# Four raw units leave the down projection for the gate and up units, and a raw unit's two dot products are parted

## The chip, the core and the metric

The kernel runs on one core of a Trainium2 chip. A core has TensorE (PE, matmul), VectorE (DVE), ScalarE (ACT), GpSimd (POOL) and SyncE (SP, which issues most DMAs here), each with its own queue of instructions, and 16 DMA engines that they share. The metric is the device time of one execution in microseconds, lower is better; the number given is the median of three runs.

## The reference

A decoder trunk of two layers on 256 tokens of width 1024, in float32. Each layer has a token mixer (convolution and retention) and a channel part: a dense SwiGLU of width 2816 in layer 0, experts in layer 1. Shift, scale and gate vectors come from a conditioning vector c. Cut to what matters here:

```python
c_act = silu(c)
for l in range(2):
    ada = c_act @ w_ada[l] + b_ada[l]          # (1024,) @ (1024, 6144)
    shift1, scale1, gate1, shift2, scale2, gate2 = split(ada, 6)
    h = x * (1 + scale1) + shift1
    x = layer_norm(alpha * x + gate1 * token_mixer(h, ...))
    h = x * (1 + scale2) + shift2
    ff = (silu(h @ w_gate) * (h @ w_up)) @ w_down      # layer 0; layer 1: experts
    x = layer_norm(alpha * x + gate2 * ff)
```

## The kernel before

The kernel streams 490 MB of weights through the core as a sequence of units. A unit is one DMA of up to 128 x 2048 float32 (1 MiB) into one of four buffers, the tile `wf` (NWF = 4), and is worked off in pieces of 128 x 1024. For each piece of a matmul unit ScalarE casts a high part (`wh`, L1696), VectorE subtracts to get the low part (`wl`, L1698), and TensorE multiplies high by high, high by low and low by high. There are six split buffers of each kind (NWS = 6).

A raw unit is not split. Those of `ada_cols` (L258) hold 2 x 1024 columns of `w_ada`, transposed: VectorE multiplies each half by silu(c), kept in `cb` on all partitions, and sums it (L264, with a short read of the accumulator), so that a raw unit is two dot products of 128 x 1024 in a row; the eighth of a group also adds a bias (L273). `ada_pair` makes eight such units for a shift and a scale vector: eight of layer 0 run in the first mixer, and sixteen of layer 1 run in the dense SwiGLU of layer 0. (The first eight of the program, made at L709, are others.)

The order of all work is written out by the program. `prog` is a list of units and code. The loop at its end (L1705) takes one piece after the other: it writes the splitting of pieces up to `look` pieces ahead (`split_to`, L1713; a raw unit counts as one piece), then what was deferred to this piece (`run_deferred`, L1714), then the piece's own work. `look` is 3 for the gate-up units and raws of the dense SwiGLU, 4 for its down units, 2 for the units `RO` of the first mixer. `issue_dma` (L1668) writes the next units' loads on SP's queue, in program order, each as soon as the unit that was issued four before it has been written as consumed: a matmul unit when its last piece is split, a raw unit behind its dot products. Which of the four buffers a load gets, and so what it waits for when it runs, is settled by the framework.

The dense SwiGLU (`ffn`, L993): two units for the first 256 columns, twenty gate-up units `GU_unit(j)`, j = 2 to 21, of two pieces each (called unit j below; 24 matmuls of 256 columns a piece), and twelve down units (22 pieces, 12 matmuls of 512 columns each). A gate-up unit ends with silu (ACT L1046), product (DVE L1047), cast (ACT L1048) and low part of the activation (DVE L1049). The raws are called raw 0 to raw 15. `weave` (L436) puts raws among the gate-up units at an even rate; the last NREST = 4 of the sixteen are kept back (L1064) and put behind the first four down units (L1072):

```python
rest = [r[0] for r in raws[len(raws) - NREST:]]
del raws[len(raws) - NREST:]
weave(units, raws, WFF)
```

In the first mixer the eight raws stand among the last gate units `F` and the units `RO`; the conv norm (`conv_ln`, L776) is deferred to the piece behind the eighth of them.

Of the kernel before, what the change touches and what calls it, by code (L numbers as in the profile page):

```python
# [17 lines left out]
ALU = mybir.AluOpType  # L18
# [4 lines left out]
D = 1024  # L23
# [46 lines left out]
COJ = 0  # L70
MS = (2, 3)
LK = {'A': 5, 'F0': 4, 'F1': 4, 'GUm': 5, 'QK0': 4, 'RO0': 2, 'D': 4}
NREST = 4
SPARE = 6
WFF = 0
START = tuple((w, k) for k in range(8) for w in "as")
# [40 lines left out]
def _emit(tc, ctx, a):  # L117
    nc = tc.nc
    pe, dve, act, pool, sp = nc.tensor, nc.vector, nc.scalar, nc.gpsimd, nc.sync
# [27 lines left out]
    class Unit:  # L147
        kind = None

        def __init__(self, src, n, fn, raw=False, look=LEAD, slot=("stream", "wf", NWF)):  # L150
            self.src, self.n, self.fn, self.raw = src, n, fn, raw
            self.look, self.slot, self.lo = look, slot, {}
            self.issued, self.before = False, None

        def width(self, s):
# [15 lines left out]
    adac = keep.tile([P, L, 48], F32, name="adac")  # L171
# [3 lines left out]
    state = {}  # L175
# [70 lines left out]
    def cook_cb():  # L246
        cb = state.pop("raw_cb", None)
        if cb is not None:
            act.activation(cb, cb, AF.Silu)
# [5 lines left out]
        dve.tensor_scalar(col("taps", 0, L * 8 * CK), col("taps", 0, L * 8 * CK), 0.5, None, op0=ALU.mult)  # L255
        act.activation(ca, col("c", 0, 8), AF.Silu)

    def ada_cols(l, n, k, done=None):  # L258
        def fn(i, w, _):
            cook_cb()  # L260
            for j in range(2):
                wj = w[:, j * D:(j + 1) * D]
                c0 = (n + j) * 8 + k
                dve.scalar_tensor_tensor(wj, wj, 1.0, state["cb"], op0=ALU.mult, op1=ALU.mult,  # L264
                                         accum_out=adac[:, l, c0:c0 + 1])
            if done is not None:
                done()
        return Unit(a["adat"][l, n // 3, k], 2048, fn, raw=True)

    def ada_pair(l, n):  # L270
        def done():
            o = adac[:, l, n * 8:n * 8 + 16]
            dve.tensor_tensor(o, o, adab[:, l, n * 8:n * 8 + 16], op=ALU.add)  # L273
        return [[ada_cols(l, n, k, done if k == 7 else None)] for k in range(8)]

    ada_open = {}

# [37 lines left out]
    def defer(k, fn):  # L315
        deferred.append([k, fn])

    def run_deferred():
        for d in list(deferred):
            d[0] -= 1  # L320
            if d[0] <= 0:
                deferred.remove(d)
                d[1]()
# [112 lines left out]
    def weave(units, raws, after=0, spare=0):  # L436
        n_units = sum(isinstance(u, Unit) and not u.raw for u in units)
        rate = min(1.0, len(raws) / max(1, n_units - after - spare))
        cnt = put = 0
        for u in units:  # L440
            prog.append(u)
            if isinstance(u, Unit) and not u.raw:
                cnt += 1
                while raws and int((cnt - after) * rate + 1e-6) > put:
                    prog.extend(raws.pop(0))
                    put += 1
        for r in raws:
            prog.extend(r)
        raws.clear()

    def mixer(l, raws, bound, fill=(), tail=()):
# [251 lines left out]
        if l == 0:  # L703
            code(open_pool)
            code(lambda: state.update(hp0=R["hp"]))
            code(setup)
            for what, k in START:
                if what == "a":
                    u = ada_cols(0, 0, k, first_h(k))  # L709
                    u.look = 0  # L710
                    if k == ROPE:
                        code(lambda: rope_tables(R["hp"]))
                else:
                    u = S_unit(k)
                prog.append(u)
            code(lambda: R.update(y=keep.tile([P, 8, T], F32, name="ycv", tag="z")))
            code(setup_late)
        else:
            first, t0, second, t1, close = bound
            prog.extend(first)  # L720
            code(t0)
            prog.extend(second)
            code(lambda: state.update(second_tile=t1))
            prog.append(V_unit(0, 0))
            prog[-1].look = 2
            if BEF[1] >= 0:
                prog[-1].before = (first + second)[BEF[1]]
            code(lambda: state.update(turned=lambda: (close(), open_pool())))
            prog.append(V_unit(0, 1))
            units += [A_unit(i) for i in range(6)]  # L730
# [262 lines left out]
    def ffn(raws, bound):  # L993
# [43 lines left out]
        def GU_unit(j):  # L1037
            def fn(s, w, wl):
                if s == 0:
                    R["g"] = mm_bank()  # L1040
                ws_block(R["g"][:, s * T:(s + 1) * T], w, wl, state["hH"], state["hL"], 0, 8, True, True)
                if s == 1:
                    ps = R["g"]
                    sg = R["p"].tile([P, T], F32, name="sg", bufs=2)
                    aa = R["p"].tile([P, T], F32, name="aa", bufs=2)
                    act.activation(sg, ps[:, 0:T], AF.Silu)  # L1046
                    dve.tensor_tensor(aa, sg, ps[:, T:2 * T], op=ALU.mult)  # L1047
                    act.copy(R["aH"][:, j, :], aa)  # L1048
                    dve.tensor_tensor(R["aL"][:, j, :], aa, R["aH"][:, j, :], op=ALU.subtract)  # L1049
            return named('GUf', Unit(a["ffn_gu"][j - 2], 2048, fn))  # L1050
# [12 lines left out]
        units = [GU_unit(j) for j in range(2, KF)]  # L1063
# [3 lines that stand above are left out]
# [564 lines left out]
    late = {}  # L1631
    ada_chunk(0, 2, gate0, lambda: late["p"].tile([P, 512], F32, name="asb", tag="tap", bufs=2))
    mixer(0, ada_pair(0, 3), None, gate0)
    ffn(ada_pair(1, 0) + ada_pair(1, 3), boundary((0, 5), 4))
    opening = []
    mixer(1, [], boundary((1, 2), 1), tail=[lambda: opening[0]()])
# [3 lines left out]
    for u in prog:  # L1640
        if isinstance(u, Unit) and u.look == LEAD and not u.raw:
            u.look = LK.get(u.kind, LEAD)
        if isinstance(u, Unit) and u.kind in LOP:
            n, r, m = LOP[u.kind]
# [13 lines left out]
    consumed = set()  # L1658
# [9 lines left out]
    def issue_dma(upto=None):  # L1668
        while st["dma"] < (len(units) if upto is None else upto):
            u = order[st["dma"]]  # L1670
            where, tag, bufs = u.slot
            p = state.get(where)
            mine = used.setdefault((where, tag, id(p)), [])
            if p is None or not st["go"] or (len(mine) >= bufs and mine[-bufs] not in consumed):
                return
            mine.append(u.idx)
            live.append(p)
            u.wf = p.tile([P, 2048], F32, name="wf", tag=tag, bufs=bufs)
            for o in range(0, u.n, 1024 if u.idx < 2 else u.n):
                o = slice(o, min(u.n, o + 1024) if u.idx < 2 else u.n)  # L1680
                sp.dma_start(u.wf[:, o], u.src[:, o])
            u.w = {}
            u.issued = True
            st["dma"] += 1

    def split_to(i, eng=dve):
        while st["split"] <= min(i, len(subs) - 1):
            u, s = subs[st["split"]]
            if not u.issued:
                return  # L1690
            if not u.raw:
                w = stream.tile([P, 1024], F32R, name="wh", tag="wh", bufs=NWS)
                wl = stream.tile([P, 1024], F32R, name="wl", tag="wl", bufs=NWS)
                m = u.width(s)
                src = u.wf[:, s * 1024:s * 1024 + m]
                act.copy(w[:, 0:m], src)  # L1696
                eng = u.lo.get(s, eng)
                eng.tensor_tensor(wl[:, 0:m], src, w[:, 0:m], op=ALU.subtract)  # L1698
                u.w[s] = (w, wl)
                if s == u.pieces() - 1:  # L1700
                    consumed.add(u.idx)
            st["split"] += 1
            issue_dma()

    for it in prog:  # L1705
        if not isinstance(it, Unit):
            it()
            issue_dma()
            continue
        for s in range(1 if it.raw else it.pieces()):  # L1710
            i = pos_of[it.idx, s]
            st["cur"] = i
            split_to(i + it.look if st["hold"] is None else min(i + it.look, st["hold"] + NWS - 1))  # L1713
            run_deferred()  # L1714
            if it.raw:
                it.fn(0, it.wf, None)
                consumed.add(it.idx)
                issue_dma()
            else:
                it.fn(s, *it.w[s])  # L1720

# [107 lines left out]
```

## Time and profile before

| | |
|---|---|
| median of 3 runs | 1744.8 us (1744.21 to 1747.59) |
| the profiled execution: time | 1747.31 us |
| the profiled execution: span | 1745.4 us |
| TensorE busy | 1693.2 us (97%) |
| VectorE busy | 1548.4 us (89%) |
| ScalarE busy | 1159.6 us (66%) |
| mean granted TensorE clock | 0.991 |
| DMA, mean over the span | 282 GB/s |

The page gives each engine's busy time; a busy TensorE is not TensorE at its peak, since matmuls overlap. Where it matters what holds TensorE up, the views to read are those of one stretch: the windows (busy time of each engine in it), the waits (who waited for whom) and the timeline (each instruction, with the idle time before it and what ended that). In this execution the gate-up units run from about 399 to 514 us, the down units from 514 to 575 us, and the raws of the first mixer from 258 to 313 us.

### The profile page before, as it was taken

Reading aid. Unit: us, or ns where it says so; the run is one execution under the profiler, and the core shown is the slowest. Engines: PE = TensorE matmul, PEld = TensorE weight load, DVE = VectorE, ACT = ScalarE, POOL = GpSimd, SP = SyncE. Lnnn points to the kernel's source line nnn. Section 1 sums busy time; section 2 is a strip of 40 time slices with the busy share of each in tenths; the row PEclk is TensorE's granted clock in tenths of the full one; section 3 lists DMA queues with packets and bytes.
Section 4 is the critical chain, followed back from the end, with each engine's and each line's share of the span. In section 5 each row is a group of like instructions: output and inputs, shape, how many; then the busy total and the mean of one; then the engine's idle time right before and its main releaser. Section 6 shows DMA issues by size and latency. Waiting matters only on the chain. (4 is left out here: it accounts for less than half of the span.)

```text
span 1745.4 us, 23910 instructions
## 1 busy us (share of the span) xinstructions
PE 1693.2 (97%) x8896; PEld 1424.0 (82%) x8896; DVE 1548.4 (89%) x2144; ACT 1159.6 (66%) x1634; POOL 53.3 (3%) x50
## 2 busy tenths in 40 slices
PE   6999999999999999999999999999999999999996
PEld 5988877669997798888887788888888888887885
DVE  7699989877787779999878999899999999898996
ACT  3566787644444565667645878778887878787783
POOL 5300000000000000000000000000000000000001
PEclk8999999999999999999999999999999999999998
DMA  9644458876789544455577799899998999898892
GB/s 358 260 164 161 166 208 295 309 294 230 299 303 353 205 171 161 154 192 174 189 301 290 304 333 389 306 383 361 370 363 329 382 354 383 310 393 308 323 351 86
DMA packets 71389, 491.59 MB, mean 282 GB/s; under 512 B 7985, under 2 KB 8753, under 8 KB 14178
## 3 DMA queue, kind: packets, MB, share of 16 engines
q1 hardware_dynamic: 69410, 484.29, 74.0%
q0 software_dynamic: 1568, 5.45, 0.9%
q8 instruction: 72, 1.18, 0.3%
q14 instruction: 51, 0.42, 0.1%
q10 hardware_dynamic: 288, 0.26, 0.0%
HBM read 488.92 MB, written 1.05 MB: 281 GB/s over the span
## 5 line engine op out<-in xcount | busy, mean ns | idle before, releaser
L1698 DVE TENSOR_TENSOR wl<-wf,wh 128x1024 fp32r<-128x1024 f32 x819 | 977.4, 1220 | 80.1 <-ACT wh L1696 66.0
L1696 ACT CAST wh<-wf 128x1024 fp32r<-128x1024 f32 x819 | 840.9, 1049 | 169.3 <-PE ps_mm L140 102.7
L140 PE MATMUL ps_mm<-wh,hgH 128*128 128x512 f32 x704 | 283.5, 403 | 0.0
L140 PE MATMUL ps_mm<-wh,hgL 128*128 128x512 f32 x704 | 275.8, 392 | 0.0
L140 PE MATMUL ps_mm<-wl,hgH 128*128 128x512 f32 x704 | 275.2, 391 | 0.2 <-DVE wl L1698 0.2
L480 ACT ACTIVATE tap<-upad,cols 128x256 f32<-128x256 f32 x300 | 129.6, 501 | 83.9 <-DVE ycv L492 83.8
L140 PE MATMUL ps_mm<-hHn,wh 128*128 128x256 f32 x576 | 163.5, 284 | 0.0
L140 PE MATMUL ps_mm<-hHn,wl 128*128 128x256 f32 x576 | 163.0, 283 | 0.0
L140 PE MATMUL ps_mm<-hLn,wh 128*128 128x256 f32 x576 | 163.0, 283 | 0.0
L140 PEld LDWEIGHTS ps_mm<-wh,hgL 128*128 128x128 f32 x704 | 132.5, 188 | 28.2
L140 PEld LDWEIGHTS ps_mm<-wl,hgH 128*128 128x128 f32 x704 | 132.9, 189 | 26.7 <-issue 1.0
L140 PEld LDWEIGHTS ps_mm<-wh,hgH 128*128 128x128 f32 x704 | 132.6, 188 | 26.0 <-issue 1.0
L140 PE MATMUL ps_mm<-wh,mb 128*128 128x512 f32 (+1 forms) x476 | 145.8, 380 | 0.0
L140 PEld LDWEIGHTS ps_mm<-hHn,wh 128*128 128x128 f32 x576 | 110.6, 192 | 0.4 <-issue 0.2
L140 PEld LDWEIGHTS ps_mm<-hLn,wh 128*128 128x128 f32 x576 | 110.6, 192 | 0.4 <-issue 0.2
L140 PEld LDWEIGHTS ps_mm<-hHn,wl 128*128 128x128 f32 x576 | 110.6, 192 | 0.0
L140 PEld LDWEIGHTS ps_mm<-wh,mb 128*128 128x128 f32 x476 | 87.9, 188 | 17.5 <-issue 1.5
L492 DVE TENSOR_TENSOR ycv<-ycv,tap 128x1024 f32<-128x1024 f32 (+1 forms) x90 | 93.9, 1043 | 5.6 <-ACT tap L480 4.2
L140 PE MATMUL ps_mm<-wl,mb 128*128 128x512 f32 (+1 forms) x238 | 89.8, 377 | 0.0
L140 PE MATMUL ps_mm<-wh,hHn 128*128 128x512 f32 x208 | 84.9, 408 | 0.0
L140 PE MATMUL ps_mm<-wh,hLn 128*128 128x512 f32 x208 | 81.4, 391 | 0.5 <-DVE hLn L392 0.5
L264 DVE SCALAR_TENSOR_TENSOR wf<-wf,cb 128x1024 f32<-128x1024 f32 x64 | 78.1, 1255 | 3.5 <-ACT cb L224 2.0
(306 smaller groups left out, 2851.9 us busy)
## 6 DMA issues: line engine op xcount, KB each, us to landing
wf<-moe_gu SPq DMA_DIRECT2D x176, 1024.0 KB, 7.1
wf<-moe_d SPq DMA_DIRECT2D x75, 1024.0 KB, 6.3
wf<-adat SPq DMA_DIRECT2D x31, 1024.0 KB, 5.9
wf<-ws SPq DMA_DIRECT2D x24, 1024.0 KB, 5.0
wf<-ffn_gu SPq DMA_DIRECT2D x20, 1024.0 KB, 6.1
wf<-v SPq DMA_DIRECT2D x16, 1024.0 KB, 4.9
wf<-g SPq DMA_DIRECT2D x16, 1024.0 KB, 5.0
wf<-f SPq DMA_DIRECT2D x16, 1024.0 KB, 4.9
```

The lines of the kernel that those rows point to most:

```text
L140: pe.matmul(out, lhsT, rhs, start=start, stop=stop)
L264: dve.scalar_tensor_tensor(wj, wj, 1.0, state["cb"], op0=ALU.mult, op1=ALU.mult, accum_out=adac[:, l, c0:c0 + 1])
L480: act.activation(t[:, c - c0, :], u[:, c, j:j + T], AF.Copy, scale=taps[:, c, j:j + 1])
L492: dve.tensor_tensor(y, y, prod[j][:, 0:n, :], op=ALU.add)
L1696: act.copy(w[:, 0:m], src)
L1698: eng.tensor_tensor(wl[:, 0:m], src, w[:, 0:m], op=ALU.subtract)
```

## The change

NREST becomes 0: all sixteen raws are woven among the gate-up units, none stands beside the down units, and the fetch of the gate's bias (L1074) comes behind the first down unit. The units made by `ada_pair` (the eight of the first mixer, too) are marked as parted: the first dot product stands where the unit stands, the second is deferred to the next piece, and the unit counts as consumed only behind that.

```diff
-NREST = 4
+NREST = 0
...
-    def ada_cols(l, n, k, done=None):
+    def ada_cols(l, n, k, done=None, parted=False):
+        def part(w, j, u):
+            wj = w[:, j * D:(j + 1) * D]
+            c0 = (n + j) * 8 + k
+            dve.scalar_tensor_tensor(wj, wj, 1.0, state["cb"], op0=ALU.mult, op1=ALU.mult,
+                                     accum_out=adac[:, l, c0:c0 + 1])
+            if j:
+                if done is not None:
+                    done()
+                if u.parted:
+                    consumed.add(u.idx)
+                    issue_dma()
+
         def fn(i, w, _):
             cook_cb()
-            for j in range(2):
-                wj = w[:, j * D:(j + 1) * D]
-                c0 = (n + j) * 8 + k
-                dve.scalar_tensor_tensor(wj, wj, 1.0, state["cb"], op0=ALU.mult, op1=ALU.mult,
-                                         accum_out=adac[:, l, c0:c0 + 1])
-            if done is not None:
-                done()
-        return Unit(a["adat"][l, n // 3, k], 2048, fn, raw=True)
+            part(w, 0, u)
+            if parted:
+                defer(1, lambda: part(w, 1, u))
+            else:
+                part(w, 1, u)
+        u = Unit(a["adat"][l, n // 3, k], 2048, fn, raw=True)
+        u.parted = parted
+        return u
...
-        return [[ada_cols(l, n, k, done if k == 7 else None)] for k in range(8)]
+        return [[ada_cols(l, n, k, done if k == 7 else None, True)] for k in range(8)]
...
             if it.raw:
                 it.fn(0, it.wf, None)
-                consumed.add(it.idx)
-                issue_dma()
+                if not it.parted:
+                    consumed.add(it.idx)
+                    issue_dma()
```

## Rows read from the trace of the kernel before

**Rows 1.** Windows: us, busy of PE, PEld, DVE, ACT, POOL; clock, DMA, GB/s.

```profile
456.00:514.00 58.00, 58.00 (x486) 58.00 (x485) 45.67 (x67) 27.11 (x40) 0.00 (x0) 1.00 0.79 292
514.00:548.00 34.00, 31.09 (x135) 24.53 (x134) 26.73 (x39) 13.08 (x15) 0.53 (x1) 1.00 0.87 322
```

**Rows 2.** Waits of PE, 395 to 600: waiter, releaser, us, times, longest.

```profile
PE ps_mm L140 <- ACT wh L1696: 1.5, 1, 1.5
PE ps_mm L140 <- DVE wl L1698: 1.4, 2, 0.8
```

**Rows 3.** Timeline of ACT, gate-up stretch: start, us, instruction, count, idle before.

```profile
445.26 0.39 ACT L1046 ACTIVATE sg<-ps_mm 128x256 f32<-128x256 f32 x1 [2.58 <-PE ps_mm L140]
...
447.09 1.99 ACT L1696 CAST wh<-wf 128x1024 fp32r<-128x1024 f32 x2
451.02 0.39 ACT L1046 ACTIVATE sg<-ps_mm 128x256 f32<-128x256 f32 x1 [1.94 <-PE ps_mm L140]
...
453.71 2.00 ACT L1696 CAST wh<-wf 128x1024 fp32r<-128x1024 f32 x2 [1.42 <-DMA wf<-ffn_gu]
```

**Rows 4.** Timeline of DVE, down stretch.

```profile
526.96 2.36 DVE L1698 TENSOR_TENSOR wl<-wf,wh 128x1024 fp32r<-128x1024 f32 x2 [3.60 <-ACT wh L1696]
529.24 1.22 DVE L264 SCALAR_TENSOR_TENSOR wf<-wf,cb 128x1024 f32<-128x1024 f32 x1
```

**Rows 5.** Timeline of DVE, beginning of the gate-up stretch.

```profile
407.14 2.36 DVE L1698 TENSOR_TENSOR wl<-wf,wh 128x1024 fp32r<-128x1024 f32 x2 [0.53 <-ACT wh L1696]
...
415.24 1.22 DVE L264 SCALAR_TENSOR_TENSOR wf<-wf,cb 128x1024 f32<-128x1024 f32 x1
```

**Rows 6.** Timeline of SP's DMA issues, gate-up stretch.

```profile
409.53 0.33 SPq L1681 DMA_DIRECT2D wf<-ffn_gu  x1
416.50 0.33 SPq L1681 DMA_DIRECT2D wf<-adat  x1
...
445.30 0.33 SPq L1681 DMA_DIRECT2D wf<-adat  x1
446.44 0.33 SPq L1681 DMA_DIRECT2D wf<-ffn_gu  x1
```

**Rows 7.** Timeline of DVE, one raw unit, the activation, the next low parts.

```profile
442.90 1.22 DVE L264 SCALAR_TENSOR_TENSOR wf<-wf,cb 128x1024 f32<-128x1024 f32 x1
...
444.04 1.22 DVE L264 SCALAR_TENSOR_TENSOR wf<-wf,cb 128x1024 f32<-128x1024 f32 x1
...
446.33 0.41 DVE L1047 TENSOR_TENSOR aa<-sg,ps_mm 128x256 f32<-128x256 f32 x1
447.21 0.42 DVE L1049 TENSOR_TENSOR aL<-aa,aH 128x256 fp32r<-128x256 f32 x1 [0.47 <-ACT aH L1048]
448.16 2.36 DVE L1698 TENSOR_TENSOR wl<-wf,wh 128x1024 fp32r<-128x1024 f32 x2 [0.53 <-ACT wh L1696]
```

**Rows 8.** The page's DMA issues: count, KB each, median us to landing.

```profile
wf<-f SPq DMA_DIRECT2D x16, 1024.0 KB, 4.9
```

**Rows 9.** One gate-up load by tile: its issue, its time to landing.

```profile
L1681 SPq DMA_DIRECT2D wf<-ffn_gu x1: 328/328/328, 475.2 to 475.2; - x1
...
DMA to landing us min/median/max: 6.5/6.5/6.5
```

**Rows 10.** Timeline of SP's DMA issues, first mixer.

```profile
261.02 0.33 SPq L1681 DMA_DIRECT2D wf<-ro  x1
264.35 0.33 SPq L1681 DMA_DIRECT2D wf<-adat  x1
269.10 2.60 SPq L1681 DMA_DIRECT2D wf<-ro  x2
```

**Rows 11.** Timeline of PE, first mixer.

```profile
277.10 0.50 PE L140 MATMUL ps_mm<-wl,rH 128*128 128x512 f32 x1 [0.20 <-DVE wl L1698]
```

**Rows 12.** Waits of PE, 100 to 395.

```profile
PE ps_mm L140 <- DVE wl L1698: 1.8, 3, 0.8
...
PE ps_sc L798 <- DVE un L789: 1.2, 2, 0.8
```

More of the change, by code (lines that the diff above doesn't have):

```diff
@@ L152, in __init__ @@
             self.look, self.slot, self.lo = look, slot, {}
+            self.parted = False
             self.issued, self.before = False, None
```

## The prediction

> **What bounds the kernel now.** First I read the busy times by stretch: in the gate and up stretch TensorE is busy all the time at full clock, VectorE four fifths of it, the DMA engines moving 292 GB/s; in the down stretch TensorE has 2.9 us of 34 idle [rows 1]. TensorE's waits name them: 1.5 us for a high part, 1.4 us for low parts [rows 2]. The reader is to see that this is all that the four raw units beside the down projection cost today. Then the rhythm: the silu of a gate-up unit starts 5.76 us after that of the unit before [rows 3], so a unit is two pieces of 2.88 us of TensorE's work without a gap.
>
> **VectorE runs in the order written.** In the down stretch it stands 3.60 us before a low part whose high part is late, and the dot product written behind starts only after it [rows 4]. This decides the case, since the change writes a low part between a raw unit's two dot products.
>
> **Which buffer a load gets.** A load is issued when its buffer is free. The gate-up load at 409.53 starts as the low parts of 407.14 end (407.14 + 2.36 = 409.50), although the code lets it go only behind the first raw unit; the raw load at 416.50 starts as that raw unit's second dot product ends (415.24 + 1.22 = 416.46) [rows 5, 6]. So buffers are handed out in the order in which their last readers are written, and loads are issued in program order. I follow the new program by this rule.
>
> **Part 1, more raw units in the gate and up stretch.** With NREST at 0 the rate is 16 raws on 20 units, not 12: they stand behind units 3 to 6, 8 to 11, 13 to 16 and 18 to 21. On VectorE a dot product takes a step of 1.14 us, a low part 1.14 us, the product to the low part of the activation 0.88 us, and from there to the next low part 0.95 us [rows 7]. A unit without a raw costs 0.88 + 0.95 + 2 x 1.14 = 4.11 us, a raw 2.28 us. Five units with four raws are 5 x 4.11 + 4 x 2.28 = 29.7 us at most, against 5 x 5.76 = 28.8 us on TensorE; a dot product written straight behind the activation fills the gap of some 0.6 us before the next low part, in four of five units: 27.3 us. VectorE just fits. The fetch grows to 9 blocks of 1.05 MB in 28.8 us, 328 GB/s, about the 322 GB/s of the down stretch [rows 1]: it fits as well, barely. By work alone this part costs nothing.
>
> **Part 2, the split dot product closes a loop.** By lines 1713 and 1714 the splitting ahead is written before the deferred work. With a raw behind nearly every unit, VectorE's order becomes: first dot product of raw k, first low part of the unit two further on, second dot product of raw k, second low part. The gate-up load that takes raw k's buffer is the one whose first low part is written ahead of raw k+1's second dot product. So that dot product frees a buffer, the load lands, the high part is cast, the low part made, and only then the next second dot product runs and frees the next buffer. From start to start of second dot products:
> - a link: 1.22 + 0.03 us to the issue [rows 5, 6]; 4.9 us for a single load to land [rows 8]; 0.05 us to the cast; 1.07 us from cast to low part (447.09 to 448.16) and 1.14 us for it [rows 3, 7]. Sum 8.4 us against 5.76 us: once the lead is used up, each link delays TensorE by 2.7 us.
> - a cycle of five units has two links; one step whose load was issued earlier, after another's low part (1.14 + 1.14 + 0.88 + 0.95 + 3 x 1.14 = 7.5 us); and one whose load is issued some 1.1 us behind another and lands 6.5 us later [rows 9]: 1.25 + 6.5 + 0.05 + 1.07 + 1.14 = 10.0 us. The cycle takes 2 x 8.4 + 7.5 + 10.0 = 34.3 us against 28.8 us: 5.5 us late.
>
> The first cycle has lead. Unit 6 takes raw 0's buffer, free at about 416.5 as before [rows 5]: its first low part is ready at 416.5 + 4.9 + 0.05 + 1.07 + 1.22 = 423.8. TensorE wants it 0.2 us into unit 6, which begins four units before the silu of 445.26, at 422.2 [rows 3]: 1.3 us late. Unit 7 adds 2.7 us, then come three cycles of 5.5 us, the last of them ending in the first down unit, which takes raw 13's buffer. Sum 1.3 + 2.7 + 16.5 = 20.5 us. Bounds: the load behind another has also taken 7.3 us (446.44 to the cast at 453.71) [rows 3, 6], which adds 3 x 0.8 = 2.4 us; 0.3 us less in each of eight links takes off 2.4 us. So 18.1 to 22.9 us.
>
> The Trainium skill's page "DMA: Bandwidth & Descriptors" (Anatomy of one DMA) fits a transfer by 2.0 us and its bytes at 436 GB/s, an estimate of 4.4 us for such a block. The median here is 4.9 us [rows 8], so the measurement decides; by the page a link would be 7.9 us and the whole of this part some 15 us.
>
> **Part 3, the down stretch.** No raws stand there. The 2.9 us of waits [rows 1, 2] go, and no other is behind them: its loads then have nothing between them, and the look ahead is four pieces. The gate's bias is fetched by POOL behind the first down unit, not the fifth; it still waits for the last dot product, and its reader is in the next layer: nothing. The adds on 16 columns move with their raws: nothing. -2.9 us.
>
> **Part 4, the eight raws of the first mixer are split too.** In most places the low parts are already written, and the halves stay adjacent. At the first two they part: the load of 261.02 now takes the buffer that comes free at 264.35, and the next moves from 269.10 to about 272.8, as it follows low parts that wait for that load [rows 10]. It lands near 277.7, its low part is ready near 280.1, and TensorE, which got it at 277.10 [rows 11], comes 3.0 us late. At the end the last second half comes behind the conv norm's arithmetic, not ahead of it: 1.14 us, and TensorE waits 1.2 us there for that norm [rows 12]: -1.2 us. Net +1.8 us. Bounds: -3.0 us if that delay doesn't come, since the waits for low parts and for the norm [rows 12] are all there is to win; +4 us if the later waits are shifted whole.
>
> **Sum.** 20.5 - 2.9 + 1.8 = 19.4 us. The profiled execution (span 1745.4, time 1747.3) would come to 1766.7; the median of the runs shown is 2.5 us under it, so I forecast 1744.8 + 19.4 = 1764 us. Own range: 18.1 - 2.9 - 3.0 = +12.2 to 22.9 - 2.9 + 4 = +24.0 us, 1757 to 1769.
>
> **Rivals.**
> 1. *No loop* (not slower). The place is VectorE's order behind a raw; it decides from the point where the second dot product runs without the next unit's low part, because it is written ahead of it or because the load is early enough. Then each linked load is issued a low part and a wait sooner, and only the 2.9 us and up to 1.2 us at the conv norm change: 1744.8 - 2.9 - 1.2 = 1740.7 us, or about 1743 us if VectorE, at 27.3 of 28.8 us, gives half back. For it: raws two in a row cost TensorE nothing today [rows 1]; against it, the lines' order and the queue [rows 4].
> 2. *Loads collide*: linked loads travel behind another each time. A link is then 1.25 + 7.3 + 0.05 + 1.07 + 1.14 = 10.8 us, eight of them add 8 x 2.4 = 19 us: 1783 us. For it: ScalarE waited 1.42 us for one such load [rows 3]; against it: in the order worked out a linked load is issued some 6 us after the one before.
> 3. *Half the loop*: the look ahead of three pieces swallows one link of each pair, four of 2.7 us: 1764 - 10.8 = 1753 us. For it: today's late casts stop ScalarE, not TensorE [rows 1, 3].
>
> **How the numbers follow.** Forecast 0.70, rival 1 0.13, rival 2 0.07, rival 3 0.10. The range takes the forecast's own and reaches to rival 3 and a part of the way to rival 2: 1753 to 1772 us. About 0.2% (3.5 us) is what a measurement of this kernel can tell from no change. Rival 1 lies across that bound: 0.06 faster, 0.07 same; the other 0.87 slower.
>
> **What would show it.** In the changed kernel's trace: silus of the gate-up units with two steps near 8.4 us in each five; some 20 us of TensorE's waits for high and low parts in that stretch, where there were none; gate-up loads issued as a second dot product ends, and casts waiting for them; no wait in the down stretch behind its first unit; the conv norm's statistics ahead of the last second half. If the silus keep 5.76 us, there is no loop and rival 1 holds; if linked loads take over 6 us, rival 2; with one long step in five, rival 3.

## The result and the profile after

| | before | after |
|---|---|---|
| median of five runs | 1746.18 us (1744.21 to 1748.11) | 1775.73 us (1772.94 to 1778.46) |
| span of the profiled execution | 1745.4 us | 1772.9 us |
| TensorE busy | 1693.2 us | 1705.7 us |
| mean granted TensorE clock | 0.991 | 0.985 |

The kernel became slower by 29.5 us, a ratio of 1.0171 (95% interval 1.016 to 1.0182). The direction was forecast; the time lies 3.7 us above the upper end of the range. As a difference it is 29.5 us, against a forecast of 19.4 and at most 27.2 (1772 less the 1744.8 us from which the prediction started).

In the kernel after, the dot products are L263, and the lines behind them stand 13 higher: `wh` is L1709, `wl` L1711, silu L1059, SP's loads L1694. First the windows over the stretches of [rows 1] (columns as there) and from the silu of unit 2 to the dense network's last norm, with the like stretch of the kernel before in a fence of its own:

```profile
456.00:514.00 58.00, 52.33 (x395) 50.52 (x395) 40.59 (x61) 21.91 (x33) 0.00 (x0) 0.94 0.68 254
514.00:548.00 34.00, 28.99 (x220) 27.24 (x219) 23.88 (x35) 12.86 (x19) 0.00 (x0) 0.98 0.71 269
413.30:604.04 190.74, 176.59 (x1161) 162.50 (x1160) 129.19 (x187) 73.38 (x99) 0.53 (x1) 0.96 0.69 260
```

```profile
404.88:574.66 169.78, 166.87 (x1161) 155.75 (x1160) 129.09 (x187) 73.43 (x99) 0.53 (x1) 1.00 0.78 293
```

The dense network takes 190.74 - 169.78 = 21.0 us longer, with the same instructions: 11.2 us of it are idle time of TensorE and 9.7 us are longer busy time. The mean clock of 0.96 accounts for some 7 us of these 9.7; what the rest is was not followed. It starts 413.30 - 404.88 = 8.4 us later, which is the first mixer's part. VectorE and the DMA engines, which the change was to load more, are less busy than before. The waits of TensorE, 395 to 640 and 100 to 395, answer to [rows 2, 12]:

```profile
PE ps_mm L140 <- DVE wl L1711: 7.2, 11, 0.8
PE ps_mm L140 <- ACT wh L1709: 6.9, 6, 1.4
```

```profile
PE ps_tp L140 <- ACT asb L305: 4.7, 1, 4.7
PE ps_tp L797 <- DVE ycv L505: 2.1, 1, 2.1
PE ps_mm L140 <- DVE wl L1711: 1.6, 2, 0.9
PE ps_mm L140 <- ACT wh L1709: 1.5, 1, 1.5
```

In the dense network the waits have the names that were forecast, but come to 14.1 us where some 20 were expected; the rest of the loss there is longer busy time. In the mixer there is one that was not: 4.7 us for `asb`, the copy of the gate's rows.

**The loop in the trace.** Three views of the kernel after, one cycle: VectorE's dot products L263 with the low parts L1711 between them, SP's issues of loads, ScalarE's casts.

```profile
467.24 1.22 DVE L263 SCALAR_TENSOR_TENSOR wf<-wf,cb 128x1024 f32<-128x1024 f32 x1
...
474.50 1.23 DVE L1711 TENSOR_TENSOR wl<-wf,wh 128x1024 fp32r<-128x1024 f32 x1 [2.53 <-ACT wh L1709]
475.64 1.22 DVE L263 SCALAR_TENSOR_TENSOR wf<-wf,cb 128x1024 f32<-128x1024 f32 x1
...
483.18 1.22 DVE L263 SCALAR_TENSOR_TENSOR wf<-wf,cb 128x1024 f32<-128x1024 f32 x1
...
492.77 1.23 DVE L1711 TENSOR_TENSOR wl<-wf,wh 128x1024 fp32r<-128x1024 f32 x1 [1.37 <-ACT wh L1709]
493.91 1.22 DVE L263 SCALAR_TENSOR_TENSOR wf<-wf,cb 128x1024 f32<-128x1024 f32 x1
```

```profile
468.49 1.47 SPq L1694 DMA_DIRECT2D wf<-ffn_gu  x2
...
483.29 0.33 SPq L1694 DMA_DIRECT2D wf<-adat  x1
484.43 0.33 SPq L1694 DMA_DIRECT2D wf<-ffn_gu  x1
```

```profile
473.41 1.99 ACT L1709 CAST wh<-wf 128x1024 fp32r<-128x1024 f32 x2 [3.05 <-DMA wf<-ffn_gu]
...
491.69 2.00 ACT L1709 CAST wh<-wf 128x1024 fp32r<-128x1024 f32 x2 [1.89 <-DMA wf<-ffn_gu]
```

Read it as a chain. The second dot product of 467.24 ends at 468.46; at 468.49 the load that takes its buffer is issued; 4.92 us later, at 473.41, it is cast (the landing of [rows 8]); the low part follows at 474.50, and only then, at 475.64, the next second dot product. From start to start 8.40 us, the link that was forecast. With the 4.4 us that the prediction estimated from the Trainium skill's page "DMA: Bandwidth & Descriptors" (Anatomy of one DMA) it would be 7.9 us; the fit there is for DMAs on GpSimd's path, while these loads are issued by SP, and the measured 4.92 us decides. The step with a load issued earlier is 483.18 - 475.64 = 7.54 us (forecast 7.5). The step with a load behind another is 493.91 - 483.18 = 10.73 us (forecast 10.0): its load, 1.14 us behind a raw's, was cast 7.26 us after its issue, not 6.5.

**The clock.** TensorE's clock stays at 1.00 through 90 to 600 us of the kernel before. In the kernel after it falls at six places from 255 us on. (It also shows 0.66 from 95 to 100 us, ahead of all that was changed; some of the other runs show a fall there and some do not.) The windows of four of the six (the clock is the third column from the right; 325 to 335 us is one place):

```profile
325.00:330.00 5.00, 3.30 (x6) 1.99 (x7) 2.50 (x4) 4.75 (x10) 0.00 (x0) 0.50 1.02 433
330.00:335.00 5.00, 5.00 (x25) 4.11 (x24) 2.60 (x4) 2.80 (x6) 0.00 (x0) 0.84 0.57 203
440.00:445.00 5.00, 4.25 (x23) 4.21 (x23) 4.01 (x7) 2.33 (x5) 0.00 (x0) 0.66 0.44 144
500.00:505.00 5.00, 3.05 (x14) 2.85 (x15) 3.83 (x5) 2.27 (x3) 0.00 (x0) 0.72 0.51 175
545.00:550.00 5.00, 4.24 (x11) 3.10 (x12) 4.09 (x6) 2.32 (x5) 0.00 (x0) 0.66 0.42 131
```

0.50 is the lower of the two levels, 1.2 of 2.4 GHz. Over 255 to 600 us the missing share of the clock, in windows of 5 us, adds up to some 12 us: 5 in the mixer and 7 in the dense network. TensorE's busy time grew by 12.5 us in the whole program, by 3.8 in the mixer (143.68 us between 257.14 and 413.30, against 139.90 between 257.60 and 404.88) and by the 9.7 in the dense network. The two go together, but the one does not measure the other.

### The profile page after: what moved, and what is told of

Read it like the earlier page. It is cut to its first block, busy times and chain, and to the rows that moved or that the text cites. A ratio compares the mean times of both kernels' runs of the same rounds, so it can differ in the third digit from the quotient of the medians.

```text
span 1772.9 us, 23908 instructions
## 1 busy us (share of the span) xinstructions
PE 1705.7 (96%) x8896; PEld 1432.5 (81%) x8896; DVE 1548.4 (87%) x2144; ACT 1158.5 (65%) x1634; POOL 53.9 (3%) x50
## 5 line engine op out<-in xcount | busy, mean ns | idle before, releaser
L1711 DVE TENSOR_TENSOR wl<-wf,wh 128x1024 fp32r<-128x1024 f32 x819 | 978.8, 1222 | 108.5 <-ACT wh L1709 95.4
L1709 ACT CAST wh<-wf 128x1024 fp32r<-128x1024 f32 x819 | 840.3, 1049 | 198.9 <-PE ps_mm L140 110.6
L263 DVE SCALAR_TENSOR_TENSOR wf<-wf,cb 128x1024 f32<-128x1024 f32 x64 | 78.9, 1247 | 2.6 <-ACT cb L225 2.0
```

## The experiments

Theory A is the loop of the prediction: a gate-up load takes the buffer of a raw unit whose second dot product stands behind the low part of another such load. Its rival B: the stretch is simply too full for VectorE and the fetch. For the mixer, theory C says that the eighth raw's second half frees its buffer too late, and rival D that the first two parted raws are all of the loss. Each ratio is to runs of the kernel before on the same chip, with its 95% interval. The runs lie on three chips, on which the kernel before has medians of 1746.25, 1746.75 and 1746.86 us. A recorded ratio is not exactly that of the two medians; where the two give different losses, both are named.

### Part 1 alone: no raws beside the down projection, all whole

```diff
 (the kernel before)
-NREST = 4
+NREST = 0
```

> Only the first part of the change: all sixteen raw units among the gate-up units, each with its two dot products in a row. Theory A (the loop: a second dot product that stands behind the next unit's low part holds the buffer for the load of the unit after): no loop, the 2.9 us of TensorE's waits in the down stretch go, so 2.9 us to 0 us less than before, ratio 0.998 to 1.000. Rival B (too much for one stretch: VectorE and the DMA engines are overfilled by four more raws among the gate-up units, parted or not): most of the 21 us that the dense SwiGLU lost comes with this part alone, 10 to 21 us more, ratio 1.006 to 1.012.

1750.01 us, 1.0023 (1.0012 to 1.0033): between the two answers, in neither. So moving the raws, priced at nothing by itself, costs some 4 us net of what the down stretch was to give. The latest gate-up load there (SP, VectorE, ScalarE):

```profile
504.72 1.22 DVE L264 SCALAR_TENSOR_TENSOR wf<-wf,cb 128x1024 f32<-128x1024 f32 x1
```

```profile
505.98 0.33 SPq L1681 DMA_DIRECT2D wf<-ffn_gu  x1
```

```profile
515.18 1.99 ACT L1696 CAST wh<-wf 128x1024 fp32r<-128x1024 f32 x2 [5.62 <-DMA wf<-ffn_gu]
```

It is issued as a dot product ends (504.72 + 1.22 = 505.94) and cast 9.2 us later, with a raw's load issued at 508.82 on its way too. So even whole raws tie a gate-up load to a dot product; whether that tie or the fetch is to blame is told apart below.

### Part 2 in the dense network, with Part 1

```diff
 (the kernel after; `parted` is made an argument of ada_pair)
-    mixer(0, ada_pair(0, 3), None, gate0)
+    mixer(0, ada_pair(0, 3, False), None, gate0)
```

> The change without the parting in the first mixer: sixteen parted raws among the gate-up units. Theory A: the dense SwiGLU's own 21 us, ratio 1.012. Rival B: the same, so this run tells the two apart only together with the one that leaves the raws whole. If the stages' losses don't add up, it is away from 21 us by more than 3.

1768.17 us, 1.0114 (1.0095 to 1.0133), 20 us by the ratio and 22 by the medians, with waits of 7.7 us for high and 7.6 us for low parts in the dense network. The size fits; it doesn't yet tell A from B, as the order and the buffers change together.

### Parting without Part 1

```diff
 (the same)
-NREST = 0
+NREST = 4
```

> The dense network's raws are split, but their number beside the down projection stays at four as before; the mixer's raws stay whole. Theory A (the loop needs raws behind nearly every unit): with three raws on five units, the load that takes raw k's buffer is wanted two units later, 11.5 us after that second dot product against a link of 8.4 us, so no link binds in the gate and up stretch; in the down stretch about as many us of waits as before (2.9), or up to 4 more. 1746 to 1750 us, ratio 1.000 to 1.002, silus at 5.8 us. Rival (the parting itself costs, wherever a raw stands): twelve of the sixteen raws in the stretch give three quarters of the 20 us, 1761 us, ratio 1.009.

1757.79 us, 1.006 (1.0038 to 1.0082): 11 us, where A had said at most 4 and the rival 15. Where it is lost decides. Up to 514 us TensorE waits 1.0 us in all: twelve parted raws among the gate-up units close no loop, as A said and the rival did not. From 514 us on it waits 8.1 us, and the clock falls behind the longest wait. There (VectorE, SP, ScalarE, TensorE):

```profile
523.29 2.36 DVE L1711 TENSOR_TENSOR wl<-wf,wh 128x1024 fp32r<-128x1024 f32 x2 [2.21 <-ACT wh L1709]
```

```profile
525.67 0.33 SPq L1694 DMA_DIRECT2D wf<-ffn_d  x1
```

```profile
531.85 1.99 ACT L1709 CAST wh<-wf 128x1024 fp32r<-128x1024 f32 x2 [7.65 <-DMA wf<-ffn_d]
```

```profile
532.95 0.79 PE L140 MATMUL ps_mm<-wh,aH 128*128 128x512 f32 x1 [2.87 <-ACT wh L1709]
```

A down unit's low parts end at 525.65, the next down load is issued at 525.67, cast at 531.85, its low parts made from 532.93 on: a second loop, of low part, load and low part. It goes round twice more: loads at 535.31 and 543.88, casts at 540.40 and 548.88, so that a round takes 9.6, 8.6 and 8.5 us. I read it so: a parted raw keeps its buffer one step longer, and the down loads rotate through the buffer of the down unit just ahead. No run tested this reading by itself. I had allowed 4 us for that stretch and it took more, since I did not see the second loop. So in this run parting costs where it makes a load follow the unit that runs just before it, and hardly elsewhere.

### The same instructions, other buffers

```diff
 (the kernel of "Part 2 in the dense network")
             load_cb(R["p"])
+            S["raw"] = ExitStack()
+            state["ffnr"] = S["raw"].enter_context(tc.tile_pool(name="rawp", bufs=1))
...
         units = [GU_unit(j) for j in range(2, KF)]
+        for r in raws[:-1]:
+            r[0].slot = ("ffnr", "rw", 3)
...
         weave(units, raws, WFF)
+        code(lambda: S["raw"].close())
```

> As the run with the dense network's raws split and none beside the down projection (1768 us), VectorE's order unchanged word for word, but fifteen of the sixteen raws load into three buffers of their own, so that no gate-up load takes a raw's buffer. Theory A (the loop goes through the buffer): the steps of 8.4 us are gone, the silus come at 5.8 us again, at most one or two steps long, and the time is that of the whole raws or better, 1744 to 1751 us, ratio 0.999 to 1.003. Rival B (VectorE's order and the fetch of 328 GB/s are too much for the stretch, whichever buffer is used): the loss stays, at least 1760 us, ratio 1.008 or more.

1743.58 us, 0.9978 (0.9969 to 0.9988). Not a bound of B survives: 25 us are gone, and VectorE's instructions stand in the same order in both traces. Its windows:

```profile
456.00:514.00 58.00, 58.00 (x486) 58.00 (x485) 49.94 (x75) 26.90 (x40) 0.00 (x0) 1.00 0.85 337
514.00:548.00 34.00, 34.00 (x157) 28.33 (x156) 24.77 (x33) 15.94 (x18) 1.57 (x3) 1.00 0.87 327
```

TensorE is busy for all of both stretches, while VectorE works 49.94 of 58 us and the DMA engines move 337 GB/s, more than the stretch was said to need. The work does fit; the buffers were the whole of the loss. The edit does two things to them, though: it separates the raws' loads from the others, and it adds three buffers to the four. No run had seven buffers in one rotation, so whether the separation or the number counts is not shown. With all raws whole the answer is the same:

```diff
 (the kernel of "Part 1 alone", with the lines just shown)
```

> None beside the down projection, all raws whole (that run gave 1750.0 us), and fifteen of the dense network's raws in three buffers of their own. If the 4 us that moving the raws cost come from the same tie (a gate-up load that waits for a raw's buffer), they go and the gain of the down stretch shows: 1741 to 1745 us, ratio 0.997 to 0.999. If they come from the fetch itself (nine blocks in 28.8 us), they stay: 1748 to 1751 us, ratio 1.001 to 1.003.

1743.71 us, 0.9984 (0.9974 to 0.9994): the 4 us of Part 1 alone were the buffers as well, not the fetch, and parting as such costs nothing in the dense network. Last, the kernel before with nothing but these buffers:

```diff
 (the kernel before, with the same lines; NREST stays 4)
```

> The kernel before with nothing changed but the buffers: eleven of the twelve raws in the gate and up stretch load into three buffers of their own; four raws stay beside the down projection, all are whole. If the 3 us by which the two runs with own buffers beat the kernel before come from the empty down stretch (its 2.9 us of waits), they are not had here: 1745.5 to 1748 us, ratio 0.9995 to 1.001, waits of 1.5 and 1.4 us in the down stretch as before. If the buffers alone bring them, 1742 to 1744.5 us, ratio 0.9975 to 0.999.

1743.12 us, 0.9978 (0.9967 to 0.9988), the second of the two answers. The edit does more than the text above says: its lines stand ahead of the one that keeps four raws back, so fifteen of the sixteen raws have the buffers of their own here too, three of the four beside the down units among them. Its down stretch:

```profile
514.00:548.00 34.00, 33.99 (x153) 27.86 (x152) 31.00 (x45) 15.66 (x17) 1.58 (x3) 1.00 0.97 377
```

The 2.9 us of [rows 1, 2] go with four raws still beside the down units. So these waits, too, came from the buffers that loads had to wait for, not from the raws' work. These three kernels are the only ones of the study that are faster than the kernel before, each by 3 to 4 us, and they agree within their intervals: with these buffers it makes no difference that shows whether raws stand beside the down units.

### The mixer's raws

```diff
 (the kernel after; `parted` is made an argument of ada_pair)
-NREST = 0
+NREST = 4
...
-    ffn(ada_pair(1, 0) + ada_pair(1, 3), boundary((0, 5), 4))
+    ffn(ada_pair(1, 0, False) + ada_pair(1, 3, False), boundary((0, 5), 4))
```

> Only the eight raws of the first mixer are parted, everything in the dense SwiGLU as before. By the place of the first gate-up silu in the two traces the mixer lost 8.9 us: ratio 1.005. If the mixer's loss hangs on something later in the program, or is given back behind it: 0 to 3 us, ratio 1.000 to 1.002.

1754.12 us, 1.0038 (1.0024 to 1.0052): 6.6 us by the ratio and 7.9 by the medians, where the prediction had 1.8. Together with the dense network's loss this makes 26.5 or 29.8 us of the 29.5, so nothing large is left that only both parts together cause. Next, the eighth raw whole again:

```diff
-done if k == 7 else None, parted)] for k in range(8)]
+done if k == 7 else None, parted and k < 7)] for k in range(8)]
```

> As the run that parts the mixer's raws alone, but the eighth of them keeps its two dot products in a row, ahead of the conv norm. Theory C (the eighth's second half, written behind the conv norm, frees its buffer some 10 us later, so the first load of the convolution's output comes late, ScalarE waits for it 5.2 us, and what stands behind on ScalarE makes TensorE wait 4.7 us): the larger part goes, 3 to 4 us are left from the first two parted raws, ratio 1.002. Rival D (the loss is made by the first parted raws, whose late loads shift all that follows): 7 to 9 us are left, ratio 1.004 to 1.005.

1749.94 us, 1.0014 (1.0004 to 1.0023), 4.2 us less, and the wait for `asb` shrinks from 4.5 to 0.4 us: theory C. TensorE in this run, with the waits that are left near 279 us:

```profile
278.88 0.50 PE L140 MATMUL ps_mm<-wh,rH 128*128 128x512 f32 x1 [1.65 <-ACT wh L1709]
...
280.14 0.79 PE L140 MATMUL ps_mm<-wl,rH 128*128 128x512 f32 x1 [0.76 <-DVE wl L1711]
...
324.72 1.13 PE L140 MATMUL ps_tp<-asb,sel 128*128 128x512 f32 x2 [0.38 <-ACT asb L305]
```

Then the first two whole as well:

```diff
+done if k == 7 else None, parted and 2 <= k < 7)] for k in range(8)]
```

> The first mixer's raws split but for three, the first, the second and the eighth; the dense network as before. Rival D's place (the first two splits move the loads of the first units of the retention output): the waits of 1.65 and 0.76 us near 279 us and the fall of the clock behind them go, and 1749.9 us becomes 1745.5 to 1747 us, ratio 0.9995 to 1.0005. If other splits share the loss: 1748 to 1750 us, ratio 1.001 to 1.002.

1746.53 us, 0.9997 (0.9988 to 1.0006), another 3.4 us (3.0 by the ratios; the two runs are from different chips), and the waits of 1.65 and 0.76 us near 279 us are gone. So both places count, three raws are the whole of the mixer's loss within the interval, and the five parted ones between them cost nothing that shows.

The eighth in the kernel after, by SP, VectorE, ScalarE and TensorE:

```profile
313.03 0.33 SPq L1694 DMA_DIRECT2D wf<-ro  x1
320.03 1.19 SPq L1694 DMA_DIRECT2D wf<-co  x2
```

```profile
319.47 1.54 DVE L802 TENSOR_SCALAR un<-un,ryf,nb 128x1024 f32<-128x1024 f32 x2
320.92 1.22 DVE L263 SCALAR_TENSOR_TENSOR wf<-wf,cb 128x1024 f32<-128x1024 f32 x1
```

```profile
325.12 1.04 ACT L1709 CAST wh<-wf 128x1024 fp32r<-128x1024 f32 x1 [5.20 <-DMA wf<-co]
326.07 0.58 ACT L305 COPY asb<-ps_tp 128x512 f32<-128x512 f32 x1
```

```profile
326.70 2.08 PE L140 MATMUL ps_tp<-asb,sel 128*128 128x512 f32 x2 [4.66 <-ACT asb L305]
```

In the kernel before, by VectorE and SP:

```profile
310.95 1.22 DVE L264 SCALAR_TENSOR_TENSOR wf<-wf,cb 128x1024 f32<-128x1024 f32 x1
```

```profile
309.92 0.33 SPq L1681 DMA_DIRECT2D wf<-ro  x1
312.20 5.06 SPq L1681 DMA_DIRECT2D wf<-co  x2
```

Before, the first load of the conv's output projection, `co`, was issued as the eighth's second dot product ended (310.95 + 1.22 = 312.17), 2.3 us behind the last `ro` load. In the kernel after the second half runs at 320.92, behind the conv norm that ends with `un`. The first `co` load no longer waits for it: it waits 6.6 us for TensorE, which frees the buffer of a unit of the gate, and is issued at 320.03, 7.0 us behind the last `ro` load. ScalarE stands 5.20 us before the cast of it, with the copy `asb` queued behind the cast, and TensorE waits 4.66 us for that copy.

### The clock by itself

Where TensorE waits for `asb`, four matmuls on data that is ready, into a bank that the next matmul overwrites.

```diff
 (the kernel with the mixer's raws parted)
+                        if (l, n, half) == (0, 2, 0):
+                            for _ in range(4):
+                                mm(pb, sel, x[:, 0, 0:512], True, True)
                         mm(pb, sel, asb, True, True)
```

> As the run with only the mixer's raws split (1754.1 us), with four more matmuls of 1.2 us on data that is ready, into the bank that the matmul behind them overwrites, just where TensorE waits 4.6 us for the copy of the gate's rows. They add 4.7 us of work and stand in the wait's place. Theory (TensorE's clock falls after such a wait): the granted clock stays at 1.00 in the 15 us from there on, where it was 0.70 and 0.62, and the stretch gets 1.5 to 2.0 us shorter; 1752 us, ratio 1.0025 to 1.0035. Rival (the slow matmuls there have another cause, the late load): the clock there falls as before and the time stays at 1754 us or gains the 0.2 us by which the added work is longer.

1752.23 us, 1.0029 (1.0019 to 1.004), 1.9 us less than without them (1.6 by the ratios; the two runs are from different chips), though they only add work. The four took 3.60 us in the trace, not 4.7, and 1.23 us of the wait are left. The wait and the two windows behind it, first without, then with them:

```profile
328.19 2.08 PE L140 MATMUL ps_tp<-asb,sel 128*128 128x512 f32 x2 [4.55 <-ACT asb L305]
...
325.00:330.00 5.00, 1.81 (x3) 0.84 (x3) 2.90 (x5) 3.33 (x7) 0.00 (x0) 0.70 1.00 421
330.00:335.00 5.00, 5.00 (x17) 3.92 (x16) 3.00 (x5) 2.63 (x5) 0.00 (x0) 0.62 0.73 283
```

```profile
326.07 1.12 PE L140 MATMUL ps_tp<-asb,sel 128*128 128x512 f32 x2 [1.23 <-ACT asb L305]
...
325.00:330.00 5.00, 3.93 (x17) 2.91 (x17) 2.83 (x5) 4.87 (x11) 0.00 (x0) 1.00 1.00 411
330.00:335.00 5.00, 5.00 (x28) 4.25 (x27) 3.79 (x8) 4.88 (x10) 0.00 (x0) 1.00 0.65 233
```

The clock stays at 1.00, and the same matmul, with its data as late as before, takes 1.12 us instead of 2.08. So the slow matmuls behind a wait are the clock, and this wait costs more than its own length: about 2 us on top.

## Why the prediction was right and wrong

The timeline splits the 29.4 us by which the dense network's last norm is later (604.04 against 574.66). The silus of units 2, 6 and 21 in the kernel after:

```profile
413.30 0.38 ACT L1059 ACTIVATE sg<-ps_mm 128x256 f32<-128x256 f32 x1 [2.45 <-PE ps_mm L140]
...
440.34 0.38 ACT L1059 ACTIVATE sg<-ps_mm 128x256 f32<-128x256 f32 x1
...
545.65 0.38 ACT L1059 ACTIVATE sg<-ps_mm 128x256 f32<-128x256 f32 x1
```

| step | forecast | measured | read from |
|---|---|---|---|
| first cycle, units 2 to 6 | +4.0 | +4.0 | silus 413.30, 440.34 against 4 x 5.76 |
| three cycles, units 6 to 21 | +16.5 | +18.9 | silus 475.31, 510.30, 545.65 against 15 x 5.76 |
| down stretch | -2.9 | -1.9 | silu of unit 21 to the norm: 58.39 against 60.28 |
| first mixer | +1.8 | +8.9 | silu of unit 2, 8.4 us later, though the mixer began 0.45 us earlier (a raw's load at 257.14, before 257.60) |

**Right: Part 2, the closed loop.** Its place, its order, the link of 8.4 us and the lead of the first cycle are in the trace to a tenth of a microsecond, and the run with other buffers shows that the buffers are the cause. Rivals 1 and 3, no loop and half of it, fall: each cycle has both long links. Rival 2 falls as stated, as linked loads land in 4.9 us. One sign failed: TensorE's waits came to 14.1 us, not some 20.

**Mis-sized in Part 2: the load behind another**, 7.26 us to its cast where I took 6.5. I had the other row, 7.3 us [rows 3, 6], and put it into the bounds. Nothing in the two rows said which to take: both loads were issued 1.1 us behind a raw's (446.44 behind 445.30, and that of [rows 9], 475.23, behind 474.10), so 6.5 was a choice. In the three cycles it measured 7.04, 7.26 and 7.48 us. The cycles came out at 35.0, 35.0 and 35.4 us rather than 34.3, and this stretch at its upper bound.

**The step that failed: Part 4.** That the last second half comes behind the conv norm was written down, but only as a gain of 1.2 us for the norm. That it also holds its buffer until then, and that a load stands behind it which ScalarE and TensorE wait for, was not followed, though it is the same rule as in Part 2. The bounds, -3.0 to +4 us, thus left out the largest cost, and the whole part came to +8.9 us in the timeline instead of +1.8. The eighth raw measured 4.2 us in the runs, net of the gain at the norm, which did come: the kernel after has no wait for `un`. The first two raws, priced at 3.0 us, measured 3.4. That this is so near is in part luck: the waits there are 1.65 and 0.76 us, and the rest goes with a clock of 0.66 from 280 to 285 us, which was not in the sum.

**Not in the sum: the clock.** Each late load was priced by its wait alone. In the dense network this does little harm, since the loop and not TensorE sets the pace and a slow TensorE fills time that it would have idled. In the mixer, and at the first down unit, where the clock of 0.66 follows the last link, it does add: by the windows it can, with the last link's wait of 0.76 us at 546.11, account for the 1.0 us by which the down stretch gave back less than forecast, though no run tested that place.

**Incomplete: Part 1.** "By work alone this part costs nothing" was true and not the question. Alone it cost 4 us, by loads that waited for raws' buffers; with other buffers it cost nothing. For the same reason the 2.9 us of waits in the down stretch were not the price of the four raws there, as the prediction's first paragraph says: with other buffers the waits went and the raws stayed.

**Not settled.** The rule that buffers are handed out in the order in which the last readers are written held in the loop, but not for the first `co` load, which got a buffer that TensorE frees. I could tell from the trace what it waited for, not why it got that one. (The load that did follow the eighth's second half is the next one of the gate, at 322.18, as that half ends at 322.14. The profile leaves out which of the four buffers a load takes; that is read from what the load waits for.) Nor is it settled whether the gain of the last three dense runs comes from separate buffers or from more of them.

## What to carry to other kernels

When work that frees a buffer is moved behind other work, follow the buffer: who loads into it next, who reads that, and whether that reader stands ahead of the next such release on the same engine; if so, the time of one round of load, cast and release sets the pace, however idle the engines are. TensorE's waits for low parts did not tell here whether the stretch was full or tied; giving the moved units buffers of their own, with not one of VectorE's instructions reordered, told it in one run, though not whether fewer shared buffers would have done. Price a wait of TensorE with the clock that may fall behind it.

## What the runs showed of the hardware that was not expected

TensorE's clock fell to the lower level not only behind the one long wait of 4.66 us but behind two short ones: 1.43 us at 439.54 and 0.76 us at 440.80 are followed by a window at 0.50 from 440.80 to 443.30. Other pairs as long passed without a fall (1.41 us at 536.44 and 0.76 us at 537.70), so the waits' length alone doesn't tell. The Trainium skill's page "TensorE: Matmul & The Clock Gate" (Part 1: The HAM clock gate) has two states of the clock gate, 1.2 GHz after idling and 2.4 GHz when busy. The trace agrees on the levels: windows lie at 1.00, at 0.50 or, where one holds both, between.

A load of 1 MiB took 4.9 us from its issue to its cast in the loop, where no other had been issued in the 7 us before it (468.49 to 473.41), though one followed 1.14 us later. Gate-up loads issued 1.14 us behind another landed after 6.2 to 7.6 us in the kernel after (those at 469.63 and 513.01). One took 9.2 us to its cast between two raws' loads (issued at 501.92 and 508.82, in the run with Part 1 alone).
